# A gate vector summed over partitions: turning transfers and VectorE additions in place of an fp32 product with ones

## The chip, the core and the metric

One core of a Trainium2 chip runs the whole kernel. Its engines work side by side: TensorE (PE; its weight loads are shown apart as PEld), VectorE (DVE), ScalarE (ACT), GpSimd (POOL), and SyncE (SP), which here only issues transfers. Each of them runs its instructions in a fixed order and waits on semaphores for the others. On-chip memory (SBUF) has 128 partitions; TensorE writes to a second memory, PSUM. The metric is the device time of one execution in microseconds, the median of several runs.

## What is computed

One layer of a conditioned decoder: RMS norm, a scale and shift that depend on a conditioning vector `c`, a gated short convolution, an output projection, a gated residual, and a final RMS norm. All data are fp32; 256 tokens, model width 2048, branch width 4096.

```python
def adaln(h, c, w, b):
    mod = jnp.einsum('bd,df->bf', jax.nn.silu(c), w) + b
    shift, scale, gate = jnp.split(mod, 3, axis=-1)
    h = h * (1.0 + scale[:, None, :]) + shift[:, None, :]
    return h, gate

def short_conv_mixer(h, w_in, conv_w, w_out):
    proj = jnp.einsum('bsd,de->bse', h, w_in)
    b_gate, c_gate, v, g = jnp.split(proj, 4, axis=-1)
    u = causal_depthwise_conv(c_gate * v, conv_w)
    y = b_gate * u * jax.nn.silu(g)
    return jnp.einsum('bse,ed->bsd', y, w_out)
...
    x = x + gate[:, None, :] * y
    return rmsnorm(x, final_g)
```

The change is about `gate`: 2048 values, each a sum over the 2048 entries of silu(c) times a column of `ada_w`.

## The kernel before

**The large products.** Every weight block is loaded raw in fp32 and split into two parts, `hi` (a cast by ScalarE, line 341) and `lo` (raw minus hi, by VectorE, line 346), and each product is made of three: hi times the tokens' hi, hi times their lo, lo times their hi (line 471). Raw, hi and lo have three buffers each, used in turn: a cast waits until TensorE is through with the block three places earlier. SP's queue loads the blocks.

**The stages.** In the first (tile names `mm_s`, `raw_s`), the first half of the branch is projected while the scale and shift are still being summed (`ada_piece`, tiles `at`, `gv`). In the second (`mm_b`, `raw`, lines 626 to 660), the other half follows in eight pairs of column tiles, pairs 8 to 15; each pair goes through the four quarters of `w_in` in the order q = 1, 2, 3, 0, with two weight blocks of 8 x 128 rows for each quarter. The third stage is the output projection (`mm_w`, `mm_o`, `raw_o`, line 695), and at its end the gate, the residual and the norm.

**The gate.** It is summed in four blocks of 512 columns (`dc`). A `gate_piece` is called behind each weight block of the second stage, and 32 calls do it all: each loads two slices of 128 rows of `ada_w` (tile `at_g`, line 584, on SP's queue) and adds them, each partition's row times its entry of silu(c), to `gacc` (lines 591 and 593, VectorE). Behind the last piece of a block `gacc` holds 128 partial rows, and their sum over the partitions is wanted on every partition. TensorE makes it, as a product of an all-ones matrix with `gacc` in fp32 (line 596), and VectorE adds it to `gate(dc)` (line 597), which was filled with the bias by a broadcast load (line 563). The gates are read at lines 703 and 815, in the third stage.

**The order.** Nothing here is ordered by hand: a planner that works through a list by priority puts each engine's instructions in order before the run, from its own estimates of durations. The gate's pieces carry a lower priority (`later(GIVE)`), so that they fill what is free and may run long ahead of their place in the code. Tiles come from pools with a fixed number of buffers: `gacc` (tag `gv`) has two, `at_g` (tag `at`) four, shared in turn with the tiles of `token_forms`, and the 20 large `slots` go in turn to x, the accumulators, y, the gates and finally `zs[0]` and `zs[1]`, which get the last that come free. In the second stage `zs[0][:, 1]` keeps the evicted bank of q = 1, `zs[1]` those of q = 2 and 3, and the halves of all four serve again at the end. `zs[0][:, 0]` holds only the sums of `token_forms` (lines 604 to 624), which is called for pairs 10 to 15; the forms of pair 14 take both `gv` buffers.

Of the kernel before, what the change touches and what calls it, by code (L numbers as in the profile page):

```python
# [8 lines left out]
F32 = mybir.dt.float32  # L9
F32R = mybir.dt.float32r  # L10
AF = mybir.ActivationFunctionType
ALU = mybir.AluOpType

P = 128
# [103 lines left out]
def short_conv_layer(ctx: ExitStack, tc: tile.TileContext, x, c, norm_g, ada_w, ada_b, w_in, conv_w, w_out, final_g, out):  # L118
    nc = tc.nc
# [11 lines left out]
    psum = ctx.enter_context(tc.tile_pool(name="psum", bufs=3, space=PSUM))  # L131
# [5 lines left out]
    def slot(shape, name, dtype=F32):  # L137
        return slots.tile(shape, dtype, tag="slot", name=name)
# [100 lines left out]
    ones = const.tile([P, 1], F32, tag="ones", name="ones")  # L239
# [35 lines left out]
    for t in range(TT):  # L275
        for dh in range(2):
# [3 lines left out]
            else:  # L280
                nc.vector.scalar_tensor_tensor(
                    out=junk[:, t], in0=xt[t][dh], scalar=1.0, in1=xt[t][dh], op0=ALU.mult, op1=ALU.mult,
# [145 lines left out]
    sums = {}  # L428
# [132 lines left out]
    zs = [slot([P, 2, 2, T], f"z{j}") for j in range(2)]  # L561
# [6 lines left out]
    def gate(dc):  # L568
        return gates[dc // 2][:, dc % 2, :]

    gate_todo = [(dc, j) for dc in range(4) for j in range(0, KT, 2)]
    gacc = [None]

    def gate_piece():
        if not gate_todo:
            return
        dc, j = gate_todo.pop(0)
        at = adap.tile([P, ASLOT], F32, tag="at", name="at_g", bufs=4)
        at3 = at.rearrange("p (k f) -> p k f", k=2)
        with later(GIVE):  # L580
            gate_sums(dc, j, at3)

    def gate_sums(dc, j, at3):
        nc.sync.dma_start(at3, adas[:, j : j + 2, 2, dc * 512 : (dc + 1) * 512])
        if j == 0:
            gacc[0] = adap.tile([P, 512], F32, tag="gv", name="gacc")
        ga = gacc[0]
        for i in range(2):
            s = silu_c[:, j + i : j + i + 1]
            if j + i == 0:  # L590
                nc.vector.tensor_scalar_mul(ga, at3[:, i, :], s)
            else:
                nc.vector.scalar_tensor_tensor(out=ga, in0=at3[:, i, :], scalar=s, in1=ga, op0=ALU.mult, op1=ALU.add)  # L593
        if j + 2 == KT:
            ps = psum.tile([P, 512], F32, tag="sm", name="ps_gate", bufs=2)
            nc.tensor.matmul(ps, ones.to_broadcast([P, P]), ga, start=True, stop=True)  # L596
            nc.vector.tensor_tensor(out=gate(dc), in0=ps, in1=gate(dc), op=ALU.add)

    KP = 8
    EP = 4  # L600
# [2 lines left out]

    def token_forms(pair, u):

        sums = zs[0][:, 0].rearrange("p a (b f) -> p (a b) f", f=P)
        a11, a12 = u[:, 0, 0:P], u[:, 1, 0:P]
        a21, a22 = u[:, 0, P:T], u[:, 1, P:T]
        s1n, s2, s3, s4 = (sums[:, j] for j in range(4))
        nc.vector.scalar_tensor_tensor(out=s1n, in0=a21, scalar=-1.0, in1=a22, op0=ALU.mult, op1=ALU.subtract)  # L610
        nc.vector.scalar_tensor_tensor(out=s2, in0=s1n, scalar=-1.0, in1=a11, op0=ALU.mult, op1=ALU.subtract)
        nc.vector.tensor_tensor(out=s3, in0=a11, in1=a21, op=ALU.subtract)
        nc.vector.tensor_tensor(out=s4, in0=a12, in1=s2, op=ALU.subtract)
        if pair < 14:
            form = adap.tile([P, ASLOT], F32R, tag="at", name="form", bufs=4).rearrange("p (h s f) -> p h s f", h=2, f=P)
            hi, lo = form[:, 0], form[:, 1]
        elif pair == 14:
            hi, lo = (adap.tile([P, 512], F32R, tag="gv", name="form_g").rearrange("p (s f) -> p s f", f=P) for _ in range(2))
        else:
            form = hpool.tile([P, 2, 4, P], F32R, tag="big2", name="form_h")  # L620
            hi, lo = form[:, 0], form[:, 1]
        forms[pair] = hi, lo
        nc.scalar.copy(hi, sums)
        nc.vector.tensor_tensor(out=lo, in0=sums, in1=hi.bitcast(F32), op=ALU.subtract)

    for ct in range(NS, NCT, 2):
        for q in QUARTERS:
# [17 lines left out]
            if q == 1:  # L645
                nc.scalar.copy(z, bank)
                zc = z
            elif q == 2:
                nc.vector.tensor_tensor(out=zc, in0=bank, in1=zc, op=ALU.mult)
                for j in range(2):  # L650
                    conv(ct + j, z[:, j, :], zc[:, j, :])
                u = z
            elif q == 3:
                nc.scalar.activation(z, bank, AF.Silu)
                nc.vector.tensor_tensor(out=u, in0=u, in1=z, op=ALU.mult)
            else:
                nc.vector.tensor_tensor(out=u, in0=bank, in1=u, op=ALU.mult)
                split_y(ys[ct // 2], u)
                if ct // 2 in SEVEN:
                    token_forms(ct // 2, u)  # L660
# [130 lines left out]
    for dc in range(2, 4):  # L791
# [16 lines left out]
        for ep in range(n_ep):  # L808
# [3 lines left out]
            if dc == 3:  # L812
# [3 lines left out]
                    out=raw3, in0=raw3, in1=gate(dc).unsqueeze(1).to_broadcast([P, EP, W]), op=ALU.mult  # L816
# [8 lines left out]
        for t in range(TT):  # L825
# [4 lines left out]
            if dc == 2:  # L830
                gated(t, dc * W, W, po[t], pr, 1)
                ps = part_sum[:, t : t + 1]
# [29 lines left out]
```

## Time and profile before

| | |
|---|---|
| median of 3 runs | 911.83 us (911.70 to 912.86) |
| the profiled execution | 911.95 us |
| its span | 910.2 us |
| granted TensorE clock | 0.997 |
| TensorE, VectorE, ScalarE, GpSimd busy | 894.2, 653.5, 476.1, 0.7 us |
| moved by DMA | 227.65 MB, 250 GB/s on average |

The span runs from the first to the last instruction; what lies around it adds 1.75 us. A row that groups instructions reads: line, engine, operation, what is written from what, count, and then the busy time with the mean of one in ns, or min/median/max in ns. In a row in order of time the first number is the start in us, the second the length; the brackets at its end give the idle time of its engine before it and what ended that. `SPq` is SP's queue: the length there is that of the issue. In a DMA row the last number is the median time in us from issue to landing. A row of stretches gives, for each engine, busy us and the number of instructions, then the granted clock, the mean busy share of the 16 DMA engines and GB/s.

### The profile page before, as it was taken

To read this page: it belongs to the slowest core of one execution; us is meant where nothing else is said; L and a number is where in the kernel's file an instruction comes from. 1 tells how busy PE (TensorE), PEld (TensorE's weight loads), DVE (VectorE), ACT (ScalarE), POOL (GpSimd) and SP (SyncE) were. 2 spreads that over 40 slices of the span, in tenths; PEclk is the share of its full clock that TensorE was granted. 3 is DMA by queue.
4 is the path that set the end of the run, shared out by engine and by line. 5 is a ranking of instruction groups with operands and counts; after the bars stand their busy time and mean duration, and the time that the engine had idled before them with its cause. 6 is when DMAs were issued, how large, how long until landed. Compare 5 with 4: busy or idle time off the path is not lost.

```text
span 910.2 us, 16272 instructions
## 1 busy us (share of the span) xinstructions
PE 894.2 (98%) x7029; PEld 854.7 (94%) x7029; DVE 653.5 (72%) x647; ACT 476.1 (52%) x422; POOL 0.7 (0%) x6
## 2 busy tenths in 40 slices
PE   6999999999999999999999999999999999999996
PEld 4999999999999999999999999999999987788885
DVE  4889899889888886665555686555555577887882
ACT  6768866665558765643333434343444335544343
POOL 0000000000000000000000000000000000000000
PEclk9999999999999999999999999999999999999998
DMA  9999999999998686676666887656666486685542
GB/s 313 367 371 349 364 309 365 346 370 359 345 327 282 184 301 189 189 241 202 202 186 186 259 273 231 201 185 194 185 193 197 137 307 191 209 293 185 185 138 93
DMA packets 159656, 227.65 MB, mean 250 GB/s; under 512 B 5680, under 2 KB 104160, under 8 KB 159200
## 3 DMA queue, kind: packets, MB, share of 16 engines
q1 hardware_dynamic: 159456, 226.56, 75.7%
q8 instruction: 55, 0.90, 0.4%
q14 instruction: 17, 0.14, 0.0%
q10 hardware_dynamic: 128, 0.04, 0.0%
HBM read 224.49 MB, written 2.10 MB: 249 GB/s over the span
## 4 chain that ended last, share of the span: by engine, by line
PE 98%; ACT 1%; DMA 1%; ACTq 0%; issue 0%; DVE 0%
PE mm_b L471 38%; PE mm_s L471 38%; PE mm_o L695 10%; PE mm_w L695 7%; PE mm L695 2%; PE tp_idle L258 1%; DMA rows<-in_ada_b_dram 1%; PE sum L380 1%; PE ps_gate L596 0%; PE tp_g L461 0%; PE tp_x L310 0%; ACT hi L341 0%; ACT acc L492 0%; ACT hT L327 0%; ACT mm_s L504 0%; ACT big L787 0%
## 5 line engine op out<-in xcount | busy, mean ns | idle before, releaser
L471 PE MATMUL mm_s<-hT,hi 128*128 128x256 f32 x2048 | 350.4, 277 | 0.1
L471 PE MATMUL mm_b<-hT,hi 128*128 128x256 f32 x2048 | 349.4, 276 | 0.0
L471 PEld LDWEIGHTS mm_s<-hT,hi 128*128 128x128 f32 x2048 | 308.5, 188 | 1.0 <-ACT hT L327 0.3
L471 PEld LDWEIGHTS mm_b<-hT,hi 128*128 128x128 f32 x2048 | 308.2, 188 | 0.5 <-issue 0.5
L471 PE MATMUL mm_b<-hT,lo 128*128 128x256 f32 x1024 | 282.6, 276 | 0.0
L471 PE MATMUL mm_s<-hT,lo 128*128 128x256 f32 x1024 | 282.2, 277 | 0.0
L346 DVE TENSOR_TENSOR lo<-raw,hi 128x2048 fp32r<-128x2048 f32 (+1 forms) x66 | 148.0, 2243 | 113.6 <-ACT hi L341 113.2
L341 ACT CAST hi<-raw 128x2048 fp32r<-128x2048 f32 (+1 forms) x66 | 123.7, 1874 | 193.9 <-PE mm_b L471 152.6
L471 PEld LDWEIGHTS mm_b<-hT,lo 128*128 128x128 f32 x1024 | 192.2, 188 | 0.5 <-issue 0.5
L471 PEld LDWEIGHTS mm_s<-hT,lo 128*128 128x128 f32 x1024 | 191.7, 188 | 0.3 <-DVE lo L346 0.2
L346 DVE TENSOR_TENSOR lo<-raw_s,hi 128x2048 fp32r<-128x2048 f32 (+1 forms) x80 | 147.6, 1850 | 32.8 <-ACT hi L341 32.0
L341 ACT CAST hi<-raw_s 128x2048 fp32r<-128x2048 f32 (+1 forms) x80 | 124.0, 1559 | 72.9 <-PE mm_s L471 59.6
L454 DVE SCALAR_TENSOR_TENSOR gv<-at,silu_c,gv 128x512 f32<-128x512 f32 x105 | 78.6, 749 | 6.3 <-DMA at<-in_ada_w_dram 4.5
L341 ACT CAST hi<-raw_o 128x2048 fp32r<-128x2048 f32 x26 | 49.6, 1906 | 60.6 <-PE mm_o L695 36.6
L695 PE MATMUL mm_o<-hi,y 128*128 128x512 f32 x256 | 78.7, 389 | 0.0
L346 DVE TENSOR_TENSOR lo<-raw_o,hi 128x2048 fp32r<-128x2048 f32 x26 | 59.5, 2290 | 24.2 <-ACT hi L341 24.1
L492 ACT COPY acc<-mm_s 128x1024 f32<-128x1024 f32 x54 | 54.6, 1012 | 34.7 <-PE mm_s L471 34.7
L695 PE MATMUL mm_w<-hi,y 128*128 128x512 f32 x184 | 58.2, 390 | 0.0
L695 PEld LDWEIGHTS mm_o<-hi,y 128*128 128x128 f32 x256 | 48.0, 188 | 9.9
L695 PE MATMUL mm_o<-lo,y 128*128 128x512 f32 x128 | 49.5, 389 | 0.0
L593 DVE SCALAR_TENSOR_TENSOR gacc<-at_g,silu_c,gacc 128x512 f32<-128x512 f32 x60 | 45.0, 749 | 5.6 <-DMA at_g<-in_ada_w_dram 4.6
L695 PEld LDWEIGHTS mm_w<-hi,y 128*128 128x128 f32 x184 | 34.5, 188 | 7.7 <-ACT hi L341 0.2
(142 smaller groups left out, 512.6 us busy)
## 6 DMA issues: line engine op xcount, KB each, us to landing
raw<-in_sc_w_in_dram SPq DMA_DIRECT2D x64, 1024.0 KB, 5.6
raw_s<-in_sc_w_in_dram SPq DMA_DIRECT2D x47, 1024.0 KB, 8.5
raw_o<-in_sc_w_out_dram SPq DMA_DIRECT2D x32, 1024.0 KB, 5.1
at<-in_ada_w_dram SPq DMA_DIRECT2D x114, 256.0 KB, 8.4
raw_s<-in_sc_w_in_dram SPq DMA_DIRECT2D x33, 512.0 KB, 6.9
at_g<-in_ada_w_dram SPq DMA_DIRECT2D x32, 512.0 KB, 7.6
at<-in_ada_w_dram SPq DMA_DIRECT2D x6, 512.0 KB, 9.4
x<-in_x_dram SPq DMA_DIRECT2D x4, 512.0 KB, 6.1
```

Source lines behind the costliest of these rows:

```text
L258: nc.tensor.matmul(tp_idle, ident, ones[:, 0:1].to_broadcast([P, 512]), start=True, stop=True)
L341: nc.scalar.copy(hi[:, :n], raw[:, :n])
L346: nc.vector.tensor_tensor(out=lo[:, :n], in0=raw[:, :n], in1=hi[:, :n].bitcast(F32), op=ALU.subtract)
L380: nc.tensor.matmul(sums0[:, o * P : (o + 1) * P], rows[:, o // NK0, (o % NK0) * P : (o % NK0 + 1) * P], col.to_broadcast([P, P]), start=k ...
L454: nc.vector.scalar_tensor_tensor(out=gv, in0=at4[:, i], scalar=c_k, in1=gv, op0=ALU.mult, op1=ALU.add)
L471: mm = last_mm[0] = nc.tensor.matmul(dst, w, h[k], start=begins and left, stop=ends, skip_group_check=True)
L492: nc.scalar.copy(acc[ch, q], bank)
L593: nc.vector.scalar_tensor_tensor(out=ga, in0=at3[:, i, :], scalar=s, in1=ga, op0=ALU.mult, op1=ALU.add)
L695: nc.tensor.matmul(dst, y[a], b, start=opens and i == 0, stop=ends and i == 2, skip_group_check=True)
```

## The change

The product with ones goes. In its place come seven steps for each of the four blocks. In a step, two transfers on Pool's queue copy `gacc` to a second tile, `turned`, with its partitions turned by `away` places (64, 32, 16, 8, 4, 2, 1), one copying the rows `away` to 127 to the start and the other the first `away` rows to the end, and VectorE adds the turned copy to `gacc`. After seven steps every partition holds the whole sum. `turned` is `zs[0][:, 0]`, and the sums of `token_forms` move to `zs[0][:, 1]`.

```diff
@@ -570,6 +570,7 @@
 
     gate_todo = [(dc, j) for dc in range(4) for j in range(0, KT, 2)]
     gacc = [None]
+    turned = zs[0][:, 0].rearrange("p a f -> p (a f)")
 
     def gate_piece():
         if not gate_todo:
@@ -592,9 +593,13 @@
             else:
                 nc.vector.scalar_tensor_tensor(out=ga, in0=at3[:, i, :], scalar=s, in1=ga, op0=ALU.mult, op1=ALU.add)
         if j + 2 == KT:
-            ps = psum.tile([P, 512], F32, tag="sm", name="ps_gate", bufs=2)
-            nc.tensor.matmul(ps, ones.to_broadcast([P, P]), ga, start=True, stop=True)
-            nc.vector.tensor_tensor(out=gate(dc), in0=ps, in1=gate(dc), op=ALU.add)
+            away = 64
+            while away:
+                nc.gpsimd.dma_start(turned[0 : P - away], ga[away:P])
+                nc.gpsimd.dma_start(turned[P - away : P], ga[0:away])
+                nc.vector.tensor_tensor(out=ga, in0=ga, in1=turned, op=ALU.add)
+                away //= 2
+            nc.vector.tensor_tensor(out=gate(dc), in0=ga, in1=gate(dc), op=ALU.add)
 
     KP = 8
     EP = 4
@@ -603,7 +608,7 @@
 
     def token_forms(pair, u):
 
-        sums = zs[0][:, 0].rearrange("p a (b f) -> p (a b) f", f=P)
+        sums = zs[0][:, 1].rearrange("p a (b f) -> p (a b) f", f=P)
         a11, a12 = u[:, 0, 0:P], u[:, 1, 0:P]
         a21, a22 = u[:, 0, P:T], u[:, 1, P:T]
         s1n, s2, s3, s4 = (sums[:, j] for j in range(4))
```

## The prediction

> **What bounds the kernel now.** I read the page's busy line and its chain of waits first, then the same chain in order of time around the instructions that the change removes.
>
> ```profile
> PE 894.2 (98%) x7029; PEld 854.7 (94%) x7029; DVE 653.5 (72%) x647; ACT 476.1 (52%) x422; POOL 0.7 (0%) x6
> ...
> PE 98%; ACT 1%; DMA 1%; ACTq 0%; issue 0%; DVE 0%
> ```
>
> TensorE holds 98% of the chain that ended last; Pool runs six instructions, all at the start. What leaves TensorE leaves the end, as long as nothing else starts to hold TensorE up. The chain by time:
>
> ```profile
> 302.94 1.72 PE ps_gate L596 x4
> 304.66 76.20 PE mm_s L471 x672
> 380.86 160.93 PE mm_b L471 x1420
> 541.79 0.86 PE ps_gate L596 x2
> 542.65 43.55 PE mm_b L471 x384
> 586.20 0.86 PE ps_gate L596 x2
> 587.05 143.74 PE mm_b L471 x1268
> ```
>
> The columns are start, length and count. The four fp32 products with ones (two passes each, so x8) stand on the path, with products of L471 unbroken on both sides. In the stretch where the new work must go, the other engines look like this:
>
> ```profile
> core 0: us, PE busy (x) PEld busy (x) DVE busy (x) ACT busy (x) POOL busy (x), PEclk, DMA share, GB/s
> 200.00:223.00 23.00, 23.00 (x205) 23.00 (x205) 20.99 (x23) 12.55 (x10) 0.00 (x0) 1.00 1.03 354
> ...
> 385.00:430.00 45.00, 45.00 (x400) 45.00 (x399) 27.24 (x25) 18.87 (x16) 0.00 (x0) 1.00 0.67 212
> 430.00:475.00 45.00, 45.00 (x400) 45.00 (x399) 22.51 (x16) 19.07 (x14) 0.00 (x0) 1.00 0.64 196
> ```
>
> From 385 to 475 us VectorE is busy 49.8 of 90 us and the DMA engines about two thirds of the time; the granted clock is 1.00.
>
> VectorE runs in an order fixed before the run, so an addition that waits for a transfer also holds the next "lo" split. How long it may do so without TensorE noticing can be read where that happens already:
>
> ```profile
> 385.46 1.17 SPq L563 DMA_DIRECT2D gate<-in_ada_b_dram  x2
> 386.22 1.91 ACT L341 CAST hi<-raw 128x2048 fp32r<-128x2048 f32 x1 [2.62 <-PE mm_b L471]
> 388.17 2.29 DVE L346 TENSOR_TENSOR lo<-raw,hi 128x2048 fp32r<-128x2048 f32 x1 [0.74 <-ACT hi L341]
> 391.66 1.91 ACT L341 CAST hi<-raw 128x2048 fp32r<-128x2048 f32 x1 [2.49 <-PE mm_b L471]
> 396.10 1.29 DVE L597 TENSOR_TENSOR gate<-ps_gate,gate 128x512 f32<-128x512 f32 x2 [4.44 <-DMA gate<-in_ada_b_dram]
> 397.31 4.49 DVE L346 TENSOR_TENSOR lo<-raw,hi 128x2048 fp32r<-128x2048 f32 x2
> ```
>
> A block is 48 products, 48 x 160.93 / 1420 = 5.44 us, and the two casts stand 5.44 us apart. Each cast is let go by the block three places ahead of its own (three buffers). So the block cast at 386.22 is due two blocks later, near 386.2 + 10.9 = 397.1, and its lo was ready at 388.17 + 2.29 = 390.5: **a lead of 6.6 us**. The addition at 396.10 kept VectorE waiting for 4.44 us, and the chain's mm_b piece runs through it unbroken. A wait below 6.6 us is free; waits that add up to more are not.
>
> **The change, part by part.** *Removed:* 1.72 + 0.86 + 0.86 = **3.44 us of TensorE on the path**. This is what the chain gives them; their modelled durations, eight of 0.59 us, would give 4.7:
>
> ```profile
> L596 PE MATMUL ps_gate<-gacc,ones x8: 590/591/592, 302.8 to 586.5; 128*128 128x512 f32 x8
> L703 DVE TENSOR_TENSOR z<-z,gate x2: 1215/1217/1219, 817.1 to 818.2; 128x1024 f32<-128x1024 f32 x2
> ```
>
> I take 3.44, and 4.7 as the far end.
>
> *Added on VectorE:* 7 additions for each of four blocks, 28 in all, both operands 128x512 fp32 in SBUF, like L655 here:
>
> ```profile
> L646 ACT COPY z<-mm_b x8: 571/573/581, 393.5 to 699.9; 128x512 f32<-128x512 f32 x8
> L655 DVE TENSOR_TENSOR z<-z x8: 682/684/685, 417.6 to 724.0; 128x512 f32<-128x512 f32 x8
> L657 DVE TENSOR_TENSOR z<-mm_b,z x8: 691/692/693, 424.4 to 730.8; 128x512 f32<-128x512 f32 x8
> L624 DVE TENSOR_TENSOR form<-z,form x4: 685/685/689, 516.1 to 648.4; 128x512 fp32r<-128x512 f32 x4
> ```
>
> 28 x 0.684 = 19.2 us, in VectorE's idle time. The last addition of each block reads SBUF instead of PSUM and costs the same.
>
> *Added on Pool's queue:* 56 transfers, two a step, which move 128 rows of 2 KB, 262 KB, together. Pool has no other work, so nothing is queued behind them there. All 28 steps move 7.3 MB; at the 354 GB/s of 200 to 223 us that is 21 us of all 16 engines, in stretches about a third free. The trace shows no transfer from Pool and none inside SBUF. The nearest rows:
>
> ```profile
> raw<-in_sc_w_in_dram SPq DMA_DIRECT2D x64, 1024.0 KB, 5.6
> at_g<-in_ada_w_dram SPq DMA_DIRECT2D x32, 512.0 KB, 7.6
> out_dram<-big SPq DMA_DIRECT2D x8, 256.0 KB, 2.9
> at<-in_ada_w_dram SPq DMA_DIRECT2D x4, 128.0 KB, 6.5
> raw<-in_sc_w_in_dram SPq DMA_DIRECT2D x2, 256.0 KB, 4.7
> rows<-in_c_dram ACTq DMA_DIRECT2D x1, 8.0 KB, 3.2
> ```
>
> So a step's pair lands after 2.9 us (a store at the end, engines half idle) to 6.5 us (engines saturated). I take 4, between the stored 256 KB and the loaded 256 KB. A step is 4 + 0.68 = 4.7 us, a rotation of seven 33 us; by the ends, 25 to 50. The Trainium skill (DMA: Bandwidth & Descriptors, on the anatomy of a transfer from Pool) fits such a transfer as 2.0 us plus bytes over 436 GB/s. That is an estimate of 2.0 to 2.6 us here, below my lower end, and a rotation of some 22 us; no run here shows one yet.
>
> *Where the rotations fall.* They need zs[0], among the last of the 20 slots handed out. The gate loads went out at 385.5 when the slots before it came free, and z is first written at 393.5, so the first rotation starts near 390, not at 303. One buffer serves all, so the second follows the first: 390 to 423 and 423 to 456.
>
> *Moved with them:* gacc has two buffers. The third block's sums, which started when the product at 302.94 let a buffer go, now wait for the first rotation:
>
> ```profile
> 303.91 0.48 DVE L591 TENSOR_SCALAR gacc<-at_g,silu_c 128x512 f32<-128x512 f32 x1
> ...
> 519.19 0.49 DVE L591 TENSOR_SCALAR gacc<-at_g,silu_c 128x512 f32<-128x512 f32 x1 [2.40 <-DMA at_g<-in_ada_w_dram]
> ```
>
> Its 12 us of VectorE (0.48 + 15 x 0.75) and four loads on SP's queue move to about 423 to 440, and its rotation to 456 to 489. VectorE from 385 to 475 then holds 49.8 + 12 + some 18 additions x 0.68 = 74 of 90 us: full, but it fits. The fourth block keeps its place (519 to 546, since its loads wait for buffers that the first token form takes) and rotates until about 579. The gates are first read at 817. The two gacc buffers go to the form of pair 14, whose u is finished at 424.4 + 6 x 43.8 = 687. Both are met with over 100 us to spare, even at 50 us a rotation. A moved at_g load that waits on SP holds the weight load behind it. That load has a similar lead: its buffer is free at 390.5, it takes 5.6 us, and its cast comes at 402.5, which leaves 6.4 us.
>
> *The other moved tile:* the token forms' sums go to the half that q = 1 writes next. L624 reads them until 516.8; the next L646 there falls at 393.5 + 3 x 43.8 = 524.9. 8 us of cover, so nothing.
>
> **Sum:** 911.95 (the profiled execution; span 910.2, 0.12 above the median of three) - 3.44 + 0 = **908.5 us**, if the additions hold no lo for more than 6.6 us.
>
> **The rivals.** *The steps land later than VectorE's order allows for (slower).* The order is drawn up from estimates; with a real step longer by d, each wait adds to the one before, since the splits stand between the additions. Three rotations almost back to back give 21d, the fourth 7d, and each group has the 6.6 us of lead once. For it: loads in this region did come late.
>
> ```profile
> DVE gacc L593 <- DMA at_g<-in_ada_w_dram: 4.6, 4, 2.0
> DVE gacc L591 <- DMA at_g<-in_ada_w_dram: 2.4, 1, 2.4
> ```
>
> Five waits of 7.0 us, 1.4 each. With d = 1.4: 21 x 1.4 - 6.6 = 22.8, 7 x 1.4 - 6.6 = 3.2, so 911.95 - 3.4 + 26 = **934.5**. It decides from 21d = 6.6 + 3.4, d = 0.48. Against it: at_g is twice the size and stands in one queue with the 1 MB weight loads, while a pair has its queue to itself; and only 5 of 32 such loads were waited for. This question carries most of the doubt.
>
> *The last steps of a rotation run on few DMA engines.* The Trainium skill (the same page, on why a DMA increments its semaphore by 16) says that a transfer spreads over the largest number up to 16 that divides its outer size, which leaves 124 rows on four engines and 127 on one, but adds that some direct copies from Pool still spread over all. As a mechanism of this kernel: one engine moves 354 / 16 / 1.03 = 21.5 GB/s, so 127 rows (260 KB) take 12.1 us on one engine where sixteen need 0.8, and 124 rows on four take 3.0. That is 11.3 + 2.2 = 13.5 us later a rotation, 6.9 beyond the lead, four times: 911.95 - 3.4 + 27.6 = **936**. Every load in the rows above has a round number of rows, so the trace neither shows nor excludes it.
>
> *The gain is not there.* TensorE reaches the later stages 3.4 us early and waits for loads or splits instead: **912**. Against it, the chain has hardly a wait in it, and the loads follow buffers that TensorE frees, so they move along with it.
>
> **Chances.** Hidden, 908.5: 0.44. Steps late: 0.32, between 914 and 950 as d goes from 0.6 to 2. Few engines: 0.14. No gain: 0.10. A difference below 0.2% (1.8 us) can't be told from none, so faster is 0.44, same 0.10 and slower 0.46. The range runs from 907 (4.7 us gained) to 936, and leaves out the upper parts of the two slow cases, some 0.17. The likeliest case's own range is 907 to 910.
>
> **What would show it.** Right: no ps_gate on TensorE, mm_b unbroken from 381 to 731 us, 56 transfers on a Pool queue from about 390 us, and VectorE's waits for them below 6 us before any one lo. The second case shows as waits of additions on those transfers at nearly every step and gaps of TensorE behind "lo" between 400 and 490 us; the third as such waits only at the last steps of each rotation. A first rotation that starts near 303 us, or sums of the third block that stay there, would break the placing; TensorE waiting past 600 us would break the sum.

## The result, and the profile after

The changed kernel takes 917.12 us (median of 7 runs, 912.05 to 918.66) against 911.72 us before (7 runs, 910.83 to 912.86): a ratio of 1.0046, 95% interval 1.003 to 1.0062. It is slower by about half a per cent, where 908.5 us was forecast. Its times also spread over 6.6 us, those of before over 2. The profiled execution took 915.49 us with a span of 913.7, 3.5 more than before.

The busy line and the chain of waits of the changed kernel's page:

```profile
PE 894.4 (98%) x7021; PEld 855.7 (94%) x7021; DVE 670.4 (73%) x675; ACT 476.1 (52%) x422; POOL 29.9 (3%) x62
...
PE 75%; DMA 15%; DVE 5%; issue 2%; POOL 1%; ACT 1%; ACTq 0%; DVEq 0%; SPq 0%
```

The eight passes are gone (7029 to 7021), VectorE has 28 instructions and 17 us more, and Pool holds the 56 transfers. The chain that was TensorE for 98% now goes through DMA and VectorE for a fifth of the span: from 390 to 589 us it follows the rotations and, between the third and the fourth, the loads and sums of the fourth block. VectorE's waits, first the one row of before, then two of after (engine, line, tile, what it waited for, total us, times, longest):

```profile
DVE lo L346 <- ACT hi L341: 181.4, 103, 3.4
```

```profile
DVE lo L346 <- ACT hi L341: 132.2, 85, 4.7
DVE gacc L600 <- DMA z<-gacc: 50.6, 24, 4.8
```

24 of the 28 additions wait for their transfers (`turned` shows as z, whose memory it is), 2.1 us each. But the waits of the lo splits for their casts shrink by 49 us. In the second stage alone they shrink by 60 us, from 113.2 to 52.9, as the rows of its splits say, first before, then after (busy us and mean ns, then the idle time before them):

```profile
L346 DVE TENSOR_TENSOR lo<-raw,hi 128x2048 fp32r<-128x2048 f32 (+1 forms) x66 | 148.0, 2243 | 113.6 <-ACT hi L341 113.2
```

```profile
L346 DVE TENSOR_TENSOR lo<-raw,hi 128x2048 fp32r<-128x2048 f32 (+1 forms) x66 | 147.7, 2239 | 53.1 <-ACT hi L341 52.9
```

So most of the waiting, the additions and the 12 us of the third block's sums, which moved here from the first stage, took the place of waiting that was there before.

The first rotation on VectorE, in order of time, and the same on Pool:

```profile
390.00 0.68 DVE L600 TENSOR_TENSOR gacc<-gacc,z 128x512 f32<-128x512 f32 x1
392.03 2.29 DVE L346 TENSOR_TENSOR lo<-raw,hi 128x2048 fp32r<-128x2048 f32 x1 [1.34 <-ACT hi L341]
397.73 0.69 DVE L600 TENSOR_TENSOR gacc<-gacc,z 128x512 f32<-128x512 f32 x1 [3.41 <-DMA z<-gacc]
398.34 2.28 DVE L346 TENSOR_TENSOR lo<-raw,hi 128x2048 fp32r<-128x2048 f32 x1
403.54 0.69 DVE L600 TENSOR_TENSOR gacc<-gacc,z 128x512 f32<-128x512 f32 x1 [2.91 <-DMA z<-gacc]
```

```profile
312.32 0.68 POOL L598 DMA_DIRECT2D z<-gacc  x1 [311.02 <-DVE acc L535]
...
390.98 0.53 POOL L598 DMA_DIRECT2D z<-gacc  x1 [77.46 <-DVE gacc L600]
391.50 0.50 POOL L599 DMA_DIRECT2D z<-gacc  x1
398.72 0.54 POOL L598 DMA_DIRECT2D z<-gacc  x1 [6.72 <-DVE gacc L600]
```

About one addition stands between each pair of lo splits. From the end of an addition it takes 0.3 us until Pool issues the first transfer and 0.53 us more until it issues the second, whose landing then counts; the seven additions of this rotation start between 390.00 and 424.36, 5.7 us a step.

During the first three rotations TensorE hardly notices: it is busy for 139.98 of the 140 us from 380 to 520. It stops later, and the row of its weight loads tells for what (before it was 0.5, for "issue"):

```profile
L471 PEld LDWEIGHTS mm_b<-hT,lo 128*128 128x128 f32 x1024 | 193.0, 188 | 4.5 <-DVE lo L346 4.5
```

The longest stop, in stretches of 2 us (after PEld come DVE, ACT, POOL, then the granted clock):

```profile
core 0: us, PE busy (x) PEld busy (x) DVE busy (x) ACT busy (x) POOL busy (x), PEclk, DMA share, GB/s
...
526.00:528.00 2.00, 0.72 (x7) 0.52 (x5) 2.00 (x2) 0.00 (x0) 0.00 (x0) 1.00 1.07 353
528.00:530.00 2.00, 1.49 (x12) 1.50 (x13) 1.93 (x4) 0.29 (x1) 0.00 (x0) 0.99 0.67 237
530.00:532.00 2.00, 2.00 (x11) 2.00 (x10) 1.64 (x3) 1.62 (x1) 0.00 (x0) 0.50 0.90 253
532.00:534.00 2.00, 2.00 (x13) 2.00 (x13) 2.00 (x2) 0.00 (x0) 0.00 (x0) 0.66 0.96 322
```

TensorE stands for 1.8 us, and then the granted clock is 0.50 and 0.66 for 4 us, which costs 2 x 0.50 + 2 x 0.34 = 1.7 us more. Three shorter stops follow up to 593 us. The stage of mm_b lasts from 379.28 to 734.25, 354.97 us; without a stop it takes 348.16 (the first experiment below). So 6.8 us are lost, of which 4.5 are weight loads waiting for lo and 1.7 the clock; 0.6 are left over. Against the 3.44 us removed that leaves the 3.5 us by which the span grew (the start adds 0.1).

What came before that stop, from the chain in order of time:

```profile
500.14 6.88 DMA z<-gacc
507.14 0.70 DVE gacc L600
...
512.55 2.30 DVE lo L346
515.28 8.73 DMA at_g<-in_ada_w_dram
524.56 0.76 DVE gacc L594
```

A late pair of the third rotation holds VectorE until 507.14 (after a wait of 4.83 us), the second lo behind it ends at 514.8, with it a raw buffer comes free for SP's next weight load, and only behind that does SP issue the fourth block's first load, at 515.28 (510.58 before). VectorE then stands with that block's first sum until 524.03 (519.19 before), and TensorE runs out at 526.7. The lo that it waits for stands behind these sums on VectorE; its cast was done at 518.96. Here it is before, and then after, with the product that waited for it:

```profile
521.33 2.29 DVE L346 TENSOR_TENSOR lo<-raw,hi 128x2048 fp32r<-128x2048 f32 x1
```

```profile
526.16 2.29 DVE L346 TENSOR_TENSOR lo<-raw,hi 128x2048 fp32r<-128x2048 f32 x1
528.51 0.39 PE L471 MATMUL mm_b<-hT,lo 128*128 128x256 f32 x1 [1.79 <-DVE lo L346]
```

This lo is 4.8 us late. Before, it was finished at 523.6, and its block, the 28th of the stage, was due at about 380.86 + 27 x 5.44 = 527.7: a lead of only some 4.1 us, because the same sums stood ahead of it there too. In the changed kernel the stage starts 1.6 us sooner, which takes as much from the lead. By this estimate TensorE had to wait about 2 us, and it waited 1.8.

### The profile page after: what moved, and what is told of

Read it like the earlier page. It is cut to its first block, busy times and chain, and to the rows that moved or that the text cites. A ratio compares the mean times of both kernels' runs of the same rounds, so it can differ in the third digit from the quotient of the medians.

```text
span 913.7 us, 16414 instructions
## 1 busy us (share of the span) xinstructions
PE 894.4 (98%) x7021; PEld 855.7 (94%) x7021; DVE 670.4 (73%) x675; ACT 476.1 (52%) x422; POOL 29.9 (3%) x62
## 4 chain that ended last, share of the span: by engine, by line
PE 75%; DMA 15%; DVE 5%; issue 2%; POOL 1%; ACT 1%; ACTq 0%; DVEq 0%; SPq 0%
PE mm_s L471 38%; PE mm_b L471 17%; DMA z<-gacc 11%; PE mm_o L700 10%; PE mm_w L700 7%; DMA at_g<-in_ada_w_dram 3%; PE mm L700 2%; DVE gacc L600 2%; DVE lo L346 2%; POOL z L598 1%; PE tp_idle L258 1%; DMA rows<-in_ada_b_dram 1%; DVE gacc L594 1%; PE sum L380 1%; PE tp_g L461 0%
## 5 line engine op out<-in xcount | busy, mean ns | idle before, releaser
L346 DVE TENSOR_TENSOR lo<-raw,hi 128x2048 fp32r<-128x2048 f32 (+1 forms) x66 | 147.7, 2239 | 53.1 <-ACT hi L341 52.9
L600 DVE TENSOR_TENSOR gacc<-gacc,z 128x512 f32<-128x512 f32 x28 | 19.4, 691 | 50.6 <-DMA z<-gacc 50.6
```

The lines of the kernel that those rows point to most:

```text
L346: nc.vector.tensor_tensor(out=lo[:, :n], in0=raw[:, :n], in1=hi[:, :n].bitcast(F32), op=ALU.subtract)
L600: nc.vector.tensor_tensor(out=ga, in0=ga, in1=turned, op=ALU.add)
```

## The experiments

Each was timed beside the kernel before, on the same chip, where the kernel before took 911.4 to 911.8 us (medians):

| | us, median (lowest to highest) | ratio to before, 95% interval |
|---|---|---|
| all additions on Pool | 908.11 (907.81 to 908.48) | 0.9965, 0.9952 to 0.9977 |
| no sum over partitions | 907.82 (907.72 to 908.26) | 0.9963, 0.995 to 0.9977 |
| additions alone | 908.06 (907.60 to 908.51) | 0.9963, 0.9951 to 0.9976 |
| transfers alone | 907.88 (907.40 to 908.39) | 0.9962, 0.995 to 0.9975 |
| first two blocks turned | 910.45 (909.71 to 911.14) | 0.9988, 0.998 to 0.9997 |
| first three turned | 915.86 (911.53 to 918.80) | 1.0042, 1.0028 to 1.0056 |
| last alone turned | 910.92 (910.60 to 911.33) | 0.9992, 0.9983 to 1.0001 |
| all but the third turned | 909.32 (908.84 to 911.72) | 0.998, 0.997 to 0.999 |
| third alone turned | 911.10 (910.03 to 911.74) | 0.9991, 0.9983 to 1.0 |
| three turned, no fourth block | 909.34 (908.27 to 911.38) | 0.9978, 0.9968 to 0.9987 |
| transfers on SP's queue | 968.58 (968.00 to 970.33) | 1.0629, 1.0616 to 1.0643 |
| the change once more | 914.83 (912.25 to 919.01) | 1.0042, 1.0027 to 1.0057 |

### Which part costs: additions moved to Pool, no sum, additions alone, transfers alone

The additions on Pool, the engine that issues the transfers:

```diff
-                nc.vector.tensor_tensor(out=ga, in0=ga, in1=turned, op=ALU.add)
+                nc.gpsimd.tensor_tensor(out=ga, in0=ga, in1=turned, op=ALU.add)
...
-            nc.vector.tensor_tensor(out=gate(dc), in0=ga, in1=gate(dc), op=ALU.add)
+            nc.gpsimd.tensor_tensor(out=gate(dc), in0=ga, in1=gate(dc), op=ALU.add)
```

> The 28 additions and the four additions to the gate run on Pool, which issues the transfers too, so VectorE waits for no turning transfer. If VectorE's waits for them (50.6 us in the changed kernel) are what keeps the lo splits back, TensorE's idle time behind lo goes and the 3.4 us of the removed products show: 908.0 to 909.5 us. If the transfers themselves cost (their traffic beside the weight loads), or the gate sums that moved to 426 us, or the moved sums of the token forms, it stays near the changed kernel: 914 to 918 us. VectorE waiting for Pool where the third block's sums start would lie between.

908.11 us: the waits, and the version that beats both kernels. In its chain the whole of mm_b is one piece:

```profile
378.33 348.16 PE mm_b L471 x3072
```

Its steps are no faster, since an addition takes twice as long on Pool; now Pool does the waiting, and nothing of TensorE's stands behind it there. The additions of the first rotation also moved, from 390 to 316 us, but those of the third, from 463 to 506, stayed near their place (477 to 512 in the changed kernel). The rows of its gacc (min/median/max in ns):

```profile
L594 DVE SCALAR_TENSOR_TENSOR gacc<-at_g,silu_c,gacc x60: 736/752/1792, 223.0 to 543.2; 128x512 f32<-128x512 f32 x60
L598 POOL DMA_DIRECT2D z<-gacc x28: 532/554/706, 311.4 to 590.7; - x28
...
L600 POOL TENSOR_TENSOR gacc<-gacc,z x28: 1287/1311/4384, 316.1 to 597.0; 128x512 f32<-128x512 f32 x28
```

The product alone, by leaving the sum out:

```diff
-            away = 64
-            while away:
-                nc.gpsimd.dma_start(turned[0 : P - away], ga[away:P])
-                nc.gpsimd.dma_start(turned[P - away : P], ga[0:away])
-                nc.vector.tensor_tensor(out=ga, in0=ga, in1=turned, op=ALU.add)
-                away //= 2
             nc.vector.tensor_tensor(out=gate(dc), in0=ga, in1=gate(dc), op=ALU.add)
```

> The sum over partitions is left out: neither product nor transfers nor additions, and the partial rows go to the gate as they are. It prices the product alone. The chain of before gave it 3.44 us, so 908.3 us against 911.7; 907.0 if the modelled durations (8 x 0.59 us) were right; 911.7 if the end doesn't follow TensorE.

907.82 against 911.43 us: 3.6 us, so 3.44 was the right size, and the end follows TensorE. The moved sums of the token forms are in this kernel too, so they cost nothing.

The additions without their transfers:

```diff
-            away = 64
-            while away:
-                nc.gpsimd.dma_start(turned[0 : P - away], ga[away:P])
-                nc.gpsimd.dma_start(turned[P - away : P], ga[0:away])
+            if dc == 0:
+                nc.gpsimd.memset(turned, 0.0)
+            for _ in range(7):
                 nc.vector.tensor_tensor(out=ga, in0=ga, in1=turned, op=ALU.add)
-                away //= 2
```

> The 28 additions stay on VectorE but add zeros that lie in the tile from the start; no transfers, so the sum over partitions is left out. If VectorE's added work (19 us) is hidden and only its waits cost, 908.3 us as without any sum. If the added work itself keeps the splits back, above 910.

908.06 us: 19 us more work on VectorE is hidden.

The transfers without the additions:

```diff
                 nc.gpsimd.dma_start(turned[0 : P - away], ga[away:P])
                 nc.gpsimd.dma_start(turned[P - away : P], ga[0:away])
-                nc.vector.tensor_tensor(out=ga, in0=ga, in1=turned, op=ALU.add)
                 away //= 2
```

> The 56 transfers stay on Pool's queue, each pair behind the one before, but nothing is added, so the sum over partitions is left out and VectorE waits for no pair except where a gacc buffer comes free. If only the waits of the additions cost, 908.3 to 909 us. If 7.3 MB beside the weight loads is what costs, 912 or more.

907.88 us: 7.3 MB beside the weight loads is hidden too. Neither part costs anything alone. Without additions the pairs ran earlier, though, none between 483 and 543 us; that transfers just ahead of the fourth block's loads are hidden as well is seen with the additions on Pool, where pairs were issued up to 501. What costs is that VectorE's additions wait for the transfers, and this first set settles it.

### Which rotations cost

In the next five kernels some blocks are turned as in the changed kernel, and the others keep the product of before:

```diff
-            away = 64
...
+            if dc < 2:
+                away = 64
...
+            else:
+                ps = psum.tile([P, 512], F32, tag="sm", name="ps_gate", bufs=2)
+                nc.tensor.matmul(ps, ones.to_broadcast([P, P]), ga, start=True, stop=True)
+                nc.vector.tensor_tensor(out=gate(dc), in0=ps, in1=gate(dc), op=ALU.add)
```

The first two blocks (`dc < 2`):

> The first two blocks are turned and added on VectorE, the last two keep the product with ones. In the changed kernel TensorE lost nothing before 526 us, so these two rotations should be free: their products (1.72 us on the chain of before) are gained, 909.5 to 910 us. If each rotation costs the same share of the loss, 6.8 / 4 x 2 = 3.4 us come on top, 913.

910.45 us, with no wait of TensorE for lo: free, and most of the 1.7 us is there, though half a microsecond less than expected. The third block's sums start at 428 us in this kernel too, so their move costs nothing by itself.

The first three (`dc < 3`):

> Three blocks are turned, the last keeps its product. In the changed kernel the third rotation ended at 511 us, where the fourth block's loads and sums begin, and TensorE's long stop (1.79 us, with a granted clock of about a half behind it) followed at 526. If lateness carried over from three rotations meets those loads, most of the loss stays: 2.6 us gained, some 5 lost, 912 to 915 us. If the fourth rotation made the loss, 909.

915.86 us: the whole loss, and the spread of the changed kernel with it (911.5 to 918.8), though there is no fourth rotation. TensorE's stops between 500 and 530 us:

```profile
510.73 0.39 PE L471 MATMUL mm_b<-hT,lo 128*128 128x256 f32 x1 [0.76 <-DVE lo L346]
529.26 0.39 PE L471 MATMUL mm_b<-hT,lo 128*128 128x256 f32 x1 [1.92 <-DVE lo L346]
```

The last alone (`dc == 3`):

> Only the fourth block is turned, the first three keep their products. If lateness has to add up over several rotations, this one is free as well: 911.4 - 0.9 = 910.6 us, at most 1 us more for the short stop at 592 us in the changed kernel. If the loss comes from the fourth rotation itself, 914 or more.

910.92 us; the fourth rotation is free as well.

Is it the number of rotations, or the place of the third? All but the third (`dc != 2`):

> Three blocks are turned again, but it is the third that keeps its product. If the loss needs the third rotation just ahead of the fourth block's loads and sums, this is faster than before: 2.6 us gained and at most 1.5 lost, 909 to 910.5 us. If it is the number of rotations, 914 to 917 as with the first three.

909.32 us with three rotations, where the other three took 915.86. VectorE waits just as long for their transfers, but the fourth block's first sum comes in time:

```profile
DVE gacc L601 <- DMA z<-gacc: 37.0, 17, 3.6
```

```profile
516.47 0.49 DVE L592 TENSOR_SCALAR gacc<-at_g,silu_c 128x512 f32<-128x512 f32 x1 [1.96 <-DMA at_g<-in_ada_w_dram]
```

With the first three turned the waits were 38.1 us in 15 and that sum started at 524.81. The total of the waits does not decide here; where they fall does. Two of the nine runs took 911.6 and 911.7, so a part of the loss can still occur.

The third alone (`dc == 2`):

> Only the third block is turned. With the first two blocks' products kept, its sums stay at 303 to 334 us and its rotation should come first, near 390 us, far from the fourth block's loads: free, 911.5 - 0.9 = 910.6 us. If something in the third block itself costs, 914 or more.

911.10 us, half a microsecond above the forecast of 910.6; the kernel before took 911.75 on this chip, and with 0.86 for the product 910.9 would be quite free. Its rotation ran from 396 to 431 us, far from the fourth block, and TensorE wasn't held up. So nothing in the third block itself costs.

Three turned, and nothing of the fourth block:

```diff
-    gate_todo = [(dc, j) for dc in range(4) for j in range(0, KT, 2)]
+    gate_todo = [(dc, j) for dc in range(3) for j in range(0, KT, 2)]
```

> The first three blocks are turned and added on VectorE; the fourth block's loads, sums and sum over partitions are left out, so that its gate is the bias alone. If the loss needs the third rotation and the fourth block's loads and sums together, it goes: 908 to 910 us. If the third rotation's lateness alone starves TensorE, as its short stop at 510 us with the first three turned suggests for a small part, 912 or more.

909.34 us: with the fourth block's loads and sums away, the same three rotations are nearly free (907.8 to 908 would be quite free). Both are needed: the lateness of the third rotation, and the fourth block's loads and sums behind it. This run takes away the loads, the waits for them and the sums at once; that it is the sums and their wait, which stand ahead of a lo, is read from the trace above.

### Another queue, and the change again

All four blocks, the transfers on SP's queue:

```diff
-                nc.gpsimd.dma_start(turned[0 : P - away], ga[away:P])
-                nc.gpsimd.dma_start(turned[P - away : P], ga[0:away])
+                nc.sync.dma_start(turned[0 : P - away], ga[away:P])
+                nc.sync.dma_start(turned[P - away : P], ga[0:away])
```

> All four blocks are turned and added on VectorE as in the changed kernel, but the transfers are issued on SP's queue. The additions wait as before, and each pair now waits for an addition with the weight loads queued behind it. If the issue and landing of Pool's transfers were the trouble, a queue that issues a load in 0.37 us instead of 0.53 gives less than the changed kernel, 909 to 913 us. If the waits are, the weight loads are held on top and it is slower, 918 to 930.

968.58 us, far beyond the 930 of the dearer case: the direction was right, the size wasn't. SP's queue in order of time, and TensorE's waits:

```profile
387.74 1.08 SPq L599 DMA_DIRECT2D z<-gacc  x1
389.13 0.44 SPq L637 DMA_DIRECT2D raw<-in_sc_w_in_dram  x1
398.38 0.56 SPq L598 DMA_DIRECT2D z<-gacc  x1
398.99 0.59 SPq L599 DMA_DIRECT2D z<-gacc  x1
400.58 0.39 SPq L637 DMA_DIRECT2D raw<-in_sc_w_in_dram  x1
```

```profile
PE mm_b L471 <- DVE lo L346: 47.6, 12, 10.8
```

The two queues now hold each other: a weight load stands behind a pair that waits for an addition on VectorE (389 to 400 us without a load), and the next addition stands behind a lo that needs such a load. Pool's queue was the right one for these transfers; the additions were on the wrong engine.

The changed kernel once more:

> The changed kernel once more, beside the one above on the same chip. Seven runs went from 912.1 to 918.7 us. If landings that differ from run to run decide how much of VectorE's lateness reaches TensorE, the spread stays: 912 to 919 us, where before keeps within 2 us.

914.83 us, 912.25 to 919.01: the spread is the kernel's own. In this execution too TensorE waits 3.7 us for lo, three times, the longest 3.1. The three sets in which the third rotation on VectorE meets the fourth block's loads, with the transfers on Pool's queue, spread over 6.6 to 7.3 us; the others over 3.1 at most. That landings which vary from run to run make the spread was not tried by itself.

## Why the prediction was wrong, point by point

- *3.44 us of TensorE removed, and the end follows:* right, 3.6 us when the sum is left out.
- *28 additions in VectorE's idle time, 7.3 MB of transfers in free DMA time, moved sums of the token forms under cover:* right, each alone.
- *A pair lands after 4 us, a step is 4.7:* the landing was right (2.3 to 6.9, median 4.3; the estimate of 2.0 to 2.6 beside it was too low), the step too short, since 0.3 us until Pool starts and 0.53 us until it issues the second transfer were left out. Steps were 5.7 us in the first rotation and 5.5 to 6.8 in the others.
- *Additions wait for nothing beyond the lead, so +0:* **the step that failed.** The sum had 0 there where the profiled execution shows 6.8 us. No single wait for a pair was above 4.8 us, so each would be free by the lead of 6.6 us. But that lead was read at 388 us and taken for the whole stage. At the lo that TensorE waited for at 526.7 only some 4.1 us were left in the kernel before, and what reached that lo was not one wait but a late third rotation and, behind it, a later wait for the fourth block's first load.
- *The placing:* the additions did start at 390.0, but by luck: the buffer in zs[0], taken for one of the last to come free, was free at 312, when Pool sent the first pair. VectorE's order put the additions at 390; on Pool the first started at 316. The third rotation was put at 456 to 489 and the fourth block's sums at 519. In fact its additions started between 477 and 511, and that block's loads go out right behind. This meeting, which the prediction didn't name, is where the time went. The prediction weighed each stall against the lead of 6.6 us by itself, and checked a step of 50 us a rotation only against the two far deadlines, the form of pair 14 and the gates.
- *The rival of late steps* had the right mechanism and sign and the wrong price. It let every wait add to the one before, 21d - 6.6. The measured mean wait of 2.1 us would by that have cost 46 us. It cost 6.8: most of the waiting replaced waits for casts, 60 us of them in the second stage, and the rest cost mostly where a burst of loads and sums followed. The gaps of TensorE that this rival put between 400 and 490 us came behind 526.
- *Few DMA engines in the last steps* is refuted by the landings. These rows of the changed kernel give KB and median us:

```profile
z<-gacc POOLq DMA_DIRECT2D x8, 128.0 KB, 3.8
z<-gacc POOLq DMA_DIRECT2D x4, 254.0 KB, 3.5
...
z<-gacc POOLq DMA_DIRECT2D x4, 248.0 KB, 4.0
...
z<-gacc POOLq DMA_DIRECT2D x4, 2.0 KB, 3.1
```

127 rows (254 KB) land in 3.5 us, not in 12 or more. What the Trainium skill adds to its rule (DMA: Bandwidth & Descriptors, on why a DMA increments its semaphore by 16), that some copies from Pool spread over the engines even with 127 rows, fits this.

## What to carry to other kernels

An instruction that waits for a short chain of transfers belongs on an engine whose queue feeds nothing urgent: the same rotations cost about half a per cent with the additions on VectorE, 6% with the transfers on SP, and nothing with all of it on Pool, although Pool adds half as fast. Slack is not a sum of waits against one lead: look at what else the engine waits for while it is late, above all at the next burst of loads and sums whose place is fixed. A stop of TensorE of some 2 us can cost nearly twice its length: behind stops of 1.8 and 1.9 us the granted clock dropped.

## What the runs showed of the hardware

- *The granted clock fell to a half after stops of 1.8 and 1.9 us* (the changed kernel, and the first three turned), and each time the clock cost about 1.7 us, as 3.4 us at half speed would; behind stops of 0.5 and 0.8 us it did not fall. Nor did it behind two stops of 1.74 and 1.69 us with the transfers on SP's queue (granted clock 1.00 for the next 9 us), while there a stop of 2.68 was followed by half speed. So a stop just under 2 us can be punished and need not be; whether its length alone decides, no run shows. The Trainium skill (TensorE: Matmul & The Clock Gate, the section on how the oscillation bites in real kernels) has it that TensorE may stand for up to about 3.4 us; these traces show a shorter stop punished.
- *Transfers from Pool of 2 KB and of 254 KB land alike,* in 3.1 and 3.5 us (medians of four; the sizes between took 3.7 to 5.6, in no order), beside a weight stream that keeps the engines about four fifths busy.
- *Pool and VectorE slow each other.* With the additions on Pool, some of Pool's took up to 4.38 us against a median of 1.31, and one of VectorE's sums 1.79 against 0.75, while none of those was over 0.76 without Pool's arithmetic. A lo split that started just behind one of Pool's additions took 3.23 us in place of 2.29, as if it had to wait for that addition's end:

```profile
575.82 1.29 POOL L600 TENSOR_TENSOR gacc<-gacc,z 128x512 f32<-128x512 f32 x1 [3.66 <-DMA z<-gacc]
576.04 3.23 DVE L346 TENSOR_TENSOR lo<-raw,hi 128x2048 fp32r<-128x2048 f32 x1 [1.14 <-ACT hi L341]
```

The Trainium skill (SBUF — State Buffer, Who interferes with whom) tells of a port that GpSimd's reads share with VectorE's operations on two SBUF inputs; the rows agree, though no run took the port apart. Nothing of it reached TensorE here.
